# Decoder step on one core: key sums in column groups, late gates from SBUF, three key-value units requested before the root, shorter head and tail, a third-order root

## The chip, the cores and the metric

One Trainium2 chip, one core of it. The metric is the device time of one execution in microseconds. The program has five engines that each run their own queue in order: TensorE (PE) for matrix products, VectorE (DVE), ScalarE (ACT), GpSimd (POOL) and SyncE (SP), which here issues nearly all transfers.

## What is computed

One step of a two-layer decoder for a prompt (16 meta tokens and 256 tokens) and eight sampled tokens, 280 columns in all, in float32. Layer 0 is an RWKV-7 mixer of width 4096 (64 heads of 64), layer 1 windowed attention with a sink per head over keys and values that both token groups compute once from the stream after layer 0. Both have a gate path. Cut to what the change touches:

```python
def rmsnorm(x, g):
    return x * rsqrt(mean(x * x, -1) + RMS_EPS) * g
...
kk = k_h * k_k                                                    # layer 0
kk = kk / maximum(sqrt(sum(kk * kk, axis=-1)), 1e-12)             # one sum per head and token
...
S_fin, y = scan(rwkv7_step, S0, (r, d, k, v, kk, b))
y = (y - mean) * rsqrt(var + GN_EPS) * gn_g + gn_b
y = y + sum(r_h * k_h * r_k, -1) * v_h
y = y.reshape(B, T, WIDTH) * silu(z)                              # the gate
h = h + y @ w_out
...
kv = rmsnorm(h, kv_norm) @ w_kv                                   # shared keys and values
...
y_prompt, y_sample = rmsnorm(h, final_norm)                       # after layer 1
```

## The kernel before

Activations lie with the feature on the partition, 128 rows to a tile, 280 columns (264 in layer 1). A large product is split in three: weights come from DRAM in units of 128x512 (`raw`, two k-tiles by 256 output columns), ACT casts a unit to a short-mantissa type (`whi`), DVE takes the difference (`wlo`), and `mm3` multiplies high by high, high by low and low by high (L207 to L209). Each of `raw`, `whi` and `wlo` has five buffers, so ACT and DVE work a few units ahead of PE.

`phase0` normalises the input: squares of 16 k-tiles (`dx`) on ACT and DVE as the chunks of x land, some added in pairs on DVE, twelve sum matmuls into `ps_ssq` (L324), Ln and Exp on ACT (L346, L347, with a table load between them), and the first products with `raw_k`. Then comes phase A, some 1290 us: products r, k, v, z in order on PE, and between them the chunked solve and state chain of layer 0. For each pair of k-tiles p0 the key sums are two full-width float32 matmuls of the squared keys against a selector (`sel`, L509 in the first four pairs, L814 in the other twelve), which add up four rows of one bank (`ps_kk`); DVE limits them (`ks`) and SP writes four rows to `kr` in DRAM. From L814 on the bank is the only one of its pool (`pp`); the low-rank products `ps_l`, which the ACT instruction `ta` (L862) reads, use the same bank.

A group's normalised output is put into `b = U[u]['bonus']`, the tiles `vT`, and written to `yd` in DRAM (L1240). For most groups the z product's epilogue reads it back (L761). For the two last gate tiles, b = 6 and 7, `gate_a` reads y from `yd` (L1356) and z from `zd`, copies eight sample columns and multiplies four planes (L1362, L1364); `gate_tiles` then casts (`ghi`, `glo`). These late gates fall among the last products `ps_o` of phase A.

`out_a` is the output product of layer 0: for each pair of columns 12 units, the sum with the stream (`hT`), scaled copies for the key-value product (`kvh`, `kvl`), and squares. In between `pump` issues the sampled tokens' state updates: a load, five DVE instructions (L1340 to L1343, 0.68 us each) and a store, at the unit numbers given to `plan_states`. The two last sums go to `ps_sta` (L1414), and ACT makes the root by Ln and Exp (L1416, L1417). `phase_b` begins with the key-value product; its units are requested by `gemm`, behind the root in the code. The scaled copies `bmh` for layer 1 (L1424) are written after it.

`out_b` is layer 1's output product. For each k-tile: sum with the stream, square, three transposes, three multiplies with the final norm's weight (L1831); at the end the sums (`pst`, L1834), `rsqrt` on DVE in ten instructions (L284 to L288), two halves of 1024 columns scaled on DVE and two on ACT, and the output transfers.

The order on each engine is set when the program is built: a planner with a model of each instruction's time issues ready work to each engine; inside `pe_order` blocks the written order holds, and `issue_after` keeps an instruction behind a named one. So an edit can move rows far from it.

## Time and profile before

| | us |
|---|---|
| median of three runs | 2161.58 |
| lowest and highest run | 2156.39, 2165.62 |
| the profiled execution | 2157.39 |
| its span | 2155.6 |
| PE, DVE, ACT busy in the span | 2102.4, 1709.1, 1260.4 |

A row of a timeline gives the start, the duration, the engine, the line of the kernel, the operation, out<-in, shapes and how many records are in it; in brackets stand the engine's idle time before it and what ended that. A float32 matmul leaves two records, one of a split product one. A matmul's duration runs past the start of the next, so PE's pace is read from starts. A row of a table by windows gives the window, its length, busy time (and instructions) of PE, weight loads, DVE, ACT and POOL, then the granted TensorE clock as a share of full speed (1.00 is 2.4 GHz, 0.50 is 1.2), the DMA engines' busy share and GB/s.

### The profile page before, as it was taken

How to read it: one execution, taken by the hardware profiler on the slowest of the kernel's cores; microseconds unless marked ns; L12 is line 12 of the kernel's file. 1: busy time of each engine (PE TensorE's matmuls, PEld its weight loads, DVE VectorE, ACT ScalarE, POOL GpSimd, SP SyncE). 2: the span in 40 equal slices, each digit the busy share in tenths (PEclk: the TensorE clock that was granted, in tenths of full speed). 3: DMA queues.
4: the chain of work that ended last, by engine and by line, in shares of the span. 5: the costliest groups of instructions: out<-in, count | busy, mean ns of one | idle time of the engine just before them, and what ended most of it. 6: DMA issues, size and time to landing. Idle time of an engine off the chain costs nothing.

```text
span 2155.6 us, 56147 instructions
## 1 busy us (share of the span) xinstructions
PE 2102.4 (98%) x21556; PEld 2001.5 (93%) x21556; DVE 1709.1 (79%) x4115; ACT 1260.4 (58%) x2756; POOL 136.4 (6%) x196
## 2 busy tenths in 40 slices
PE   9999999999999999999999999999999999999997
PEld 7999999999898898889989999999999999999997
DVE  7867867787587777888988787897888888878885
ACT  3457756576666666767666444565565565544443
POOL 0011100001010010100101000100000000000000
PEclk9999999999999999999999999999999999999999
DMA  7997667768666775677655778767545444577774
GB/s 252 310 331 244 197 197 237 207 191 274 200 177 183 249 231 168 208 217 205 199 159 199 242 231 250 238 198 232 149 136 167 153 148 137 170 216 239 230 222 133
DMA packets 277445, 448.52 MB, mean 208 GB/s; under 512 B 53352, under 2 KB 99112, under 8 KB 276784
## 3 DMA queue, kind: packets, MB, share of 16 engines
q1 hardware_dynamic: 276888, 443.89, 66.1%
q8 instruction: 169, 2.77, 0.5%
q10 hardware_dynamic: 288, 1.05, 0.1%
q14 instruction: 100, 0.82, 0.1%
HBM read 382.81 MB, written 66.15 MB: 208 GB/s over the span
## 4 chain that ended last, share of the span: by engine, by line
PE 59%; DVE 4%; DMA 2%; ACT 2%; issue 2%; SPq 0%; DVEq 0%; POOLq 0%; ACTq 0%
PE ps_z L207 5%; PE ps_z L208 5%; PE ps_z L209 5%; PE ps_ob L209 3%; PE ps_ob L208 3%; PE ps_ob L207 3%; PE ps_q L207 3%; PE ps_q L209 3%; PE ps_q L208 3%; PE ps_oa L208 2%; PE ps_oa L207 2%; PE ps_oa L209 2%; PE ps_o L207 1%; PE ps_o L209 1%; PE ps_o L208 1%
## 5 line engine op out<-in xcount | busy, mean ns | idle before, releaser
L207 PE MATMUL ps_z<-mhlm,whi_z 128*128 128x280 f32 x512 | 158.2, 309 | 1.1 <-ACT st L771 1.1
L207 PE MATMUL ps_q<-bmh,whi_qb 128*128 128x264 f32 x512 | 149.9, 293 | 0.1
L208 PE MATMUL ps_z<-mhlm,whi_z 128*128 128x280 f32 x512 | 149.6, 292 | 0.0
L209 PE MATMUL ps_z<-mhlm,wlo_z 128*128 128x280 f32 x512 | 149.5, 292 | 0.0
L207 PE MATMUL ps_z<-bmh,whi_zb 128*128 128x264 f32 x512 | 147.5, 288 | 0.0
L209 PE MATMUL ps_q<-bmh,wlo_qb 128*128 128x264 f32 x512 | 145.7, 285 | 0.6 <-DVE wlo_qb L186 0.6
L208 PE MATMUL ps_q<-bml,whi_qb 128*128 128x264 f32 x512 | 145.6, 284 | 0.0
L208 PE MATMUL ps_z<-bml,whi_zb 128*128 128x264 f32 x512 | 145.4, 284 | 0.0
L209 PE MATMUL ps_z<-bmh,wlo_zb 128*128 128x264 f32 x512 | 145.4, 284 | 0.0
L207 PE MATMUL ps_ob<-ghi,whi_ob 128*128 128x264 f32 x512 | 145.2, 284 | 0.0
L209 PE MATMUL ps_ob<-ghi,wlo_ob 128*128 128x264 f32 x512 | 144.8, 285 | 0.0
L208 PE MATMUL ps_ob<-glo,whi_ob 128*128 128x264 f32 x512 | 144.5, 283 | 0.0
L184 ACT CAST whi_ob<-raw_ob 128x512 fp32r<-128x512 f32 x128 | 79.2, 621 | 97.0 <-PE ps_ob L208 80.3
L184 ACT CAST whi_oa<-raw_oa 128x512 fp32r<-128x512 f32 x128 | 79.0, 620 | 89.7 <-PE ps_oa L208 27.1
L186 DVE TENSOR_TENSOR wlo_r<-raw_r,whi_r 128x512 fp32r<-128x512 f32 x128 | 87.2, 686 | 46.9 <-ACT whi_r L184 44.1
L207 PE MATMUL ps_v<-mhlm,whi_v 128*128 128x280 f32 x384 | 120.7, 314 | 0.0
L207 PE MATMUL ps_k<-mhlm,whi_k 128*128 128x280 f32 x384 | 120.1, 313 | 0.0
L184 ACT CAST whi_v<-raw_v 128x512 fp32r<-128x512 f32 x128 | 78.7, 618 | 64.0 <-PE ps_v L208 35.0
L184 ACT CAST whi_zb<-raw_zb 128x512 fp32r<-128x512 f32 x128 | 78.3, 620 | 62.5 <-PE ps_z L208 38.5
L186 DVE TENSOR_TENSOR wlo_v<-raw_v,whi_v 128x512 fp32r<-128x512 f32 x128 | 87.3, 687 | 34.8 <-ACT whi_v L184 31.2
L186 DVE TENSOR_TENSOR wlo_k<-raw_k,whi_k 128x512 fp32r<-128x512 f32 x112 | 76.7, 690 | 46.7 <-ACT whi_k L184 45.8
L186 DVE TENSOR_TENSOR wlo_oa<-raw_oa,whi_oa 128x512 fp32r<-128x512 f32 x128 | 87.1, 688 | 32.5 <-ACT whi_oa L184 29.5
(461 smaller groups left out, 7747.3 us busy)
## 6 DMA issues: line engine op xcount, KB each, us to landing
raw_k<-a_w_rkvz SPq DMA_DIRECT2D x128, 256.0 KB
raw_v<-a_w_rkvz SPq DMA_DIRECT2D x128, 256.0 KB
raw_r<-a_w_rkvz SPq DMA_DIRECT2D x128, 256.0 KB
raw_z<-a_w_rkvz SPq DMA_DIRECT2D x128, 256.0 KB
raw_oa<-a_w_out SPq DMA_DIRECT2D x128, 256.0 KB
raw_qb<-b_w_qz SPq DMA_DIRECT2D x128, 256.0 KB
raw_zb<-b_w_qz SPq DMA_DIRECT2D x128, 256.0 KB
raw_ob<-b_w_o SPq DMA_DIRECT2D x128, 256.0 KB
```

The source lines that it names most:

```text
L184: self.nc.scalar.copy(hi, src)
L186: return self.nc.vector.tensor_tensor(lo, src, hi.bitcast(F32), op=ALU.subtract)
L207: mm(ps, wh, xh, start=start, stop=False)
L208: mm(ps, wh, xl, start=False, stop=False)
L209: return mm(ps, wl, xh, start=False, stop=stop)
```

## The change

Seven edits. `phase0` adds more squares in pairs on DVE, so that eight sum matmuls are left. The key sums' selector has 32 columns instead of 128, and the two matmuls of a pair write rows 0 to 31 and 32 to 63 of the bank, each on its own; `ks` covers 64 rows and two transfers of two rows replace one of four. `rsqrt` takes one third-order step and one second-order step instead of three second-order ones: eight instructions for ten. The late gates multiply z with `vT` in SBUF, in three instructions for five, and groups 6 and 7 are no longer written to `yd` nor read. `out_a` requests three key-value units before the root's Ln. The state updates stand at other unit numbers. In `out_b` the last k-tile's sums stand ahead of its transposes, its multiplies with the final norm's weight are merged with the root's, and the first scaled piece is 512 columns wide. (The edit of `end_k` is that of `squares`; `gemm` takes the units that `out_a` has begun.)

```diff
@@ -263,10 +264,9 @@
-        selt = self.cp.tile([128, 130], F32, name="selt")
-        nc.gpsimd.memset(selt, 0.0)
-        dma(selt[:, 2:4], I['consts'][:, C_SEL:C_SEL + 2])
-        self.sel = [selt[:, 2:130], selt[:, 0:128]]
+        self.sel = self.cp.tile([128, 32], F32, name="selt")
+        nc.gpsimd.memset(self.sel, 0.0)
+        dma(self.sel[:, 0:2], I['consts'][:, C_SEL:C_SEL + 2])
         self.half = self.cp.tile([128, 2], F32, name="half")
@@ -282,10 +282,14 @@
         V.tensor_scalar(y.bitcast(I32), x.bitcast(I32), -0.5, 1597463007.0, op0=MU, op1=AD)
-        for i in range(3):
-            V.tensor_tensor(t, y, y, op=MU)
-            V.scalar_tensor_tensor(t, t, -0.5, x, op0=MU, op1=MU)
-            V.scalar_tensor_tensor(x if i == 2 else y, t, 1.5, y, op0=AD, op1=MU)
+        STT = V.scalar_tensor_tensor
+        V.tensor_tensor(t, y, y, op=MU)
+        V.tensor_tensor(t, t, x, op=MU)
+        STT(t, t, -10 / 3, t, op0=AD, op1=MU)
+        STT(y, t, 5.0, y, op0=AD, op1=MU)
+        V.tensor_tensor(t, y, y, op=MU)
+        STT(t, t, -27 / 1024, x, op0=MU, op1=MU)
+        STT(x, t, 9 / 16, y, op0=AD, op1=MU)
@@ -311,7 +315,7 @@
         vsq = lambda a, b: V.tensor_tensor(sq[:, a:b], xn[:, a:b, :N], xn[:, a:b, :N], op=MU)
-        add = lambda a, b: V.tensor_tensor(sq[:, a:a + 2], sq[:, a:a + 2], sq[:, b:b + 2], op=AD)
+        add = lambda a, b, n=2: V.tensor_tensor(sq[:, a:a + n], sq[:, a:a + n], sq[:, b:b + n], op=AD)
         pss, junk = (self.bank(self.pe, n) for n in ("ps_ssq", "ps_fill"))
@@ -336,13 +340,15 @@
             vsq(10, 12)
-            summed(8, 9, 10, 11)
             asq(12, 13)
             vsq(13, 14)
-            summed(12, 13)
-            asq(14, 15)
-            vsq(15, 16)
-            summed(14, 15)
+            add(12, 13, 1)
+            summed(12)
+            add(8, 10)
+            summed(8, 9)
+            asq(14, 16)
+            add(14, 15, 1)
+            summed(14)
             A.activation(rsb, pss[:, :N], AF.Ln, scale=1.0 / D, bias=self.epst)
@@ -506,10 +512,12 @@
         for j in range(2):
-            nc.tensor.matmul(pk[:, :N], self.sel[j], sqs[j], start=j == 0, stop=j == 1)
-        ks = self.ph.tile([128, N], F32, tag="ks0", name=f"ks{p0}")[:4]
-        nc.vector.tensor_scalar(ks, pk[:4, :N], 1e-24, None, op0=ALU.max)
-        nc.sync.dma_start(self.kr[p0 // 8][2 * p0 % 16:2 * p0 % 16 + 4], ks)
+            nc.tensor.matmul(pk[32 * j:32 * j + 32, :N], self.sel, sqs[j], start=True, stop=True)
+        ks = self.ph.tile([128, N], F32, tag="ks0", name=f"ks{p0}")[:64]
+        nc.vector.tensor_scalar(ks, pk[:64, :N], 1e-24, None, op0=ALU.max)
+        for j in range(2):
+            h = 2 * (p0 + j) % 16
+            nc.sync.dma_start(self.kr[p0 // 8][h:h + 2], ks[32 * j:32 * j + 2])
         if p0 == 6:
@@ -1236,7 +1246,7 @@
                                    op0=MU, op1=AD)
-            if j % 2:
+            if j % 2 and o < GZ // 2:
                 nc.sync.dma_start(self.yd[u // 2][:, 2 * (u % 2):2 * (u % 2) + 2, :L], b[:, :, :L])
@@ -1353,15 +1363,15 @@
             z = pool.tile([128, 4, N], F32, tag="gz", bufs=bufs, name=f"gz{b}")
-            nc.sync.dma_start(y[:, :, :L], self.yd[b][:, :, :L])
             nc.sync.dma_start(z, self.zd[b])
         else:
             nc.sync.dma_start(y, self.yd[b])
         ys = self.ys[:, 4 * b:4 * b + 4]
         if late:
-            nc.vector.tensor_copy(y[:, :, L:N], ys)
-            for pl in range(4):
-                nc.vector.scalar_tensor_tensor(y[:, pl], z[:, pl], 0.5, y[:, pl], op0=ALU.mult, op1=ALU.mult)
+            nc.vector.scalar_tensor_tensor(y[:, :, L:N], z[:, :, L:N], 0.5, ys, op0=ALU.mult, op1=ALU.mult)
+            for i in range(2):
+                s, v = slice(2 * i, 2 * i + 2), self.U[2 * b + i]['bonus']
+                nc.vector.scalar_tensor_tensor(y[:, s, :L], z[:, s, :L], 0.5, v[:, :, :L], op0=ALU.mult, op1=ALU.mult)
         else:
@@ -1391,7 +1401,7 @@
         self.wx = self.wx0
-        self.plan_states(self.st0, 0, range(12, 96, 7), 5)
+        self.plan_states(self.st0, 0, [*range(10, 60, 6), 74, 81, 88], 5)
         ones = pool.tile([128, 128], F32, name="ones")
@@ -1413,6 +1423,8 @@
                                  stop=k == KT - 1)
+        units = self.wunits(self.I['w_kv'][0], "kv", KT, 0, 256, 2)
+        self.kvu = itertools.chain([next(units) for _ in range(3)], units)
         nc.scalar.activation(self.rb, pst[:, :N], AF.Ln, bias=self.epst, scale=1.0 / D)
@@ -1455,7 +1467,7 @@
                 if c % 2 == 0:
-                    pss = self.gemm(I['w_kv'][0], "kv", KT, c * 128, x)
+                    pss = self.gemm(I['w_kv'][0], "kv", KT, c * 128, x, units=None if c else self.kvu)
                     self.pump(c == 2)
@@ -1797,6 +1809,10 @@
+    def stb(self, pst, rows, a, one, first):
+        for i, r in enumerate(rows):
+            self.nc.tensor.matmul(pst[i][:r, 0:2], a[:, 128 * i:128 * i + r], one, start=first, stop=not first)
+
     def out_b(self):
@@ -1824,28 +1840,37 @@
             pt = self.bank(self.pe, f"ps_h2_{k}")
+            if k == KT - 1:
+                self.stb(pst, rows, sq, one, False)
             for i, r in enumerate(rows):
                 nc.tensor.transpose(pt[:r, 128 * i:128 * i + 128], h[:, 128 * i:128 * i + r], self.ident)
-            for i, r in enumerate(rows):
+            for i, r in enumerate(rows[:3 if k < KT - 1 else 0]):
                 s = slice(128 * k, 128 * k + 128)
                 V.tensor_tensor(ht[i][:r, s], pt[:r, 128 * i:128 * i + 128], fn[:r, s], op=ALU.mult)
-            if k >= KT - 2:
-                for i, r in enumerate(rows):
-                    nc.tensor.matmul(pst[i][:r, 0:2], (acc if k == KT - 2 else sq)[:, 128 * i:128 * i + r], one,
-                                     start=k == KT - 2, stop=k == KT - 1)
+            if k == KT - 2:
+                self.stb(pst, rows, acc, one, True)
         rs = pool.tile([128, 3], F32, name="rsf")
         V.memset(rs, 1.0)
         for i, r in enumerate(rows):
             V.tensor_scalar(rs[:r, i:i + 1], pst[i][:r, 0:1], 1.0 / D, EPS, op0=ALU.mult, op1=ALU.add)
         self.rsqrt(rs, pool)
         outs = (O['y_prompt'][0, 0:128], O['y_prompt'][0, 128:256], O['y_sample'].rearrange("b o d -> (b o) d"))
-        for c in range(2):
-            s = slice(D // 2 * c, D // 2 * c + D // 2)
-            V.tensor_scalar(ht[0][:, s], ht[0][:, s], rs[:, 0:1], None, op0=ALU.mult)
-            nc.sync.dma_start(outs[0][:, s], ht[0][:, s])
+        last = slice(D - 128, D)
+        scaled = lambda i, s: V.tensor_scalar(ht[i][:, s], ht[i][:, s], rs[:, i:i + 1], None, op0=ALU.mult)
+        ends = lambda i, r: V.scalar_tensor_tensor(ht[i][:r, last], pt[:r, 128 * i:128 * i + 128], rs[:r, i:i + 1],
+                                                   fn[:r, last], op0=ALU.mult, op1=ALU.mult)
+        for a, b in ((0, 512), (512, 1280), (1280, 2048)):
+            s = slice(a, min(b, D - 128))
+            scaled(0, s)
+            if b == D:
+                ends(0, 128)
+            nc.sync.dma_start(outs[0][:, a:b], ht[0][:, a:b])
             A.activation(ht[1][:, s], ht[1][:, s], AF.Copy, scale=rs[:, 1:2])
-            nc.scalar.dma_start(outs[1][:, s], ht[1][:, s])
-        V.tensor_scalar(ht[2][:NS], ht[2][:NS], rs[:NS, 2:3], None, op0=ALU.mult)
+            if b == D:
+                ends(1, 128)
+            nc.scalar.dma_start(outs[1][:, a:b], ht[1][:, a:b])
+        V.tensor_scalar(ht[2][:NS, :D - 128], ht[2][:NS, :D - 128], rs[:NS, 2:3], None, op0=ALU.mult)
+        ends(2, NS)
         nc.sync.dma_start(outs[2], ht[2][:NS])
```

What it does to the order of instructions, in three places.

DVE, phase A, round the first key sum of the third block (`ks` frees the bank for `ps_l`; `kk` and `cl` are a product and a scan that prepare another group). Before:

```order
L999 TENSOR_TENSOR RB_11396<-ps_sc_9_11574,consts 64x2x128
L186 TENSOR_TENSOR wlo_k_12_11733<-raw_k_12_11730,whi_k_12_11732 128x512
L877 SCALAR_TENSOR_TENSOR kk_11786<-kT_11782,par,kk_11786 128x280 x2
L889 SCALAR_TENSOR_TENSOR cl_11454<-reset,cl_11454 128x272 x2
L816 TENSOR_SCALAR ks_11610<-ps_kk_11607 4x280
L186 TENSOR_TENSOR wlo_k_14_11773<-raw_k_14_11770,whi_k_14_11772 128x512
```

After:

```order
L1009 TENSOR_TENSOR RB_11392<-ps_sc_9_11568,consts 64x2x128
L824 TENSOR_SCALAR ks_11604<-ps_kk_11601 64x280
L187 TENSOR_TENSOR wlo_k_12_11728<-raw_k_12_11725,whi_k_12_11727 128x512
L887 SCALAR_TENSOR_TENSOR kk_11781<-kT_11777,par,kk_11781 128x280 x2
L899 SCALAR_TENSOR_TENSOR cl_11448<-reset,cl_11448 128x272 x2
L187 TENSOR_TENSOR wlo_k_14_11768<-raw_k_14_11765,whi_k_14_11767 128x512
```

`ks` has moved ahead of a weight difference, two products and two scans.

ACT, the last products of phase A (`ghi` is the cast of a gate tile, the two of b = 6 and b = 7; `whi_oa_1792` are the weights of the last but one product, `whi_oa_0` and on those of `out_a`). Before:

```order
L184 CAST whi_oa_1792_2_20416<-raw_oa_1792_2_20414 128x512
L184 CAST whi_oa_1792_4_20441<-raw_oa_1792_4_20439 128x512
L184 CAST ghi_20349<-gy_20340 128x1120
L184 CAST whi_oa_1792_6_20447<-raw_oa_1792_6_20445 128x512
L184 CAST whi_oa_1792_8_20477<-raw_oa_1792_8_20475 128x512
L184 CAST whi_oa_1792_10_20495<-raw_oa_1792_10_20493 128x512
L184 CAST whi_oa_1792_12_20513<-raw_oa_1792_12_20511 128x512
L184 CAST whi_oa_1792_14_20531<-raw_oa_1792_14_20529 128x512
L184 CAST whi_oa_0_20597<-raw_oa_0_20595 128x512
L184 CAST whi_oa_2_20603<-raw_oa_2_20601 128x512
L184 CAST whi_oa_4_20633<-raw_oa_4_20631 128x512
L184 CAST ghi_20404<-gy_20395 128x1120
```

After:

```order
L185 CAST whi_oa_1792_0_20360<-raw_oa_1792_0_20358 128x512
L185 CAST ghi_20325<-gy_20319 128x1120
L185 CAST whi_oa_1792_2_20388<-raw_oa_1792_2_20386 128x512
L185 CAST whi_oa_1792_4_20413<-raw_oa_1792_4_20411 128x512
L185 CAST ghi_20376<-gy_20370 128x1120
L185 CAST whi_oa_1792_6_20419<-raw_oa_1792_6_20417 128x512
L185 CAST whi_oa_1792_8_20449<-raw_oa_1792_8_20447 128x512
L185 CAST whi_oa_1792_10_20467<-raw_oa_1792_10_20465 128x512
L185 CAST whi_oa_1792_12_20485<-raw_oa_1792_12_20483 128x512
```

The cast of b = 6 has moved ahead of two weight casts and that of b = 7 ahead of eight.

ACT, the root between `out_a` and the key-value product (`rb` is the root, `bmh` a scaled copy for layer 1). Before:

```order
L1417 ACT_TABLE_LOAD
L1417 ACTIVATE rb<-rb 128x280
L1424 ACTIVATE bmh_22815<-hT,par 128x280
L1424 ACTIVATE bmh_22819<-hT,par 128x280
L1424 ACTIVATE bmh_22823<-hT,par 128x280
L184 CAST whi_kv_14_22156<-raw_kv_14_22154 128x512
L1424 ACTIVATE bmh_22827<-hT,par 128x280
L184 CAST whi_kv_0_22227<-raw_kv_0_22225 128x512
```

After:

```order
L1429 ACT_TABLE_LOAD
L1429 ACTIVATE rb<-rb 128x280
L1436 ACTIVATE bmh_22787<-hT,par 128x280
L1436 ACTIVATE bmh_22791<-hT,par 128x280
L1436 ACTIVATE bmh_22795<-hT,par 128x280
L1436 ACTIVATE bmh_22799<-hT,par 128x280
L185 CAST whi_kv_14_22135<-raw_kv_14_22133 128x512
L185 CAST whi_kv_0_22200<-raw_kv_0_22198 128x512
```

`whi_kv_14`, the eighth unit, stands behind the Exp in both, after the change behind four `bmh` instead of three; `whi_kv_0` of the next columns follows it directly.

## Rows read from the trace of the kernel before

**Rows 1.** The page, part 1: busy time, share of the span and instructions of each engine.

```profile
PE 2102.4 (98%) x21556; PEld 2001.5 (93%) x21556; DVE 1709.1 (79%) x4115; ACT 1260.4 (58%) x2756; POOL 136.4 (6%) x196
```

**Rows 2.** The forms of the key-sum matmuls (durations are shortest, median, longest, in ns), and PE's timeline round one pair of them.

```profile
L814 PE MATMUL ps_kk<-sqk,selt x48: 398/399/503, 296.7 to 806.7; 128*128 128x280 f32 x48
...
L509 PE MATMUL ps_kk<-sqp,selt x16: 397/398/399, 50.7 to 79.5; 128*128 128x280 f32 x16
...
769.76 0.29 PE L209 MATMUL ps_k<-mhlm,wlo_k 128*128 128x280 f32 x1
769.89 1.11 PE L814 MATMUL ps_kk<-sqk,selt 128*128 128x280 f32 x4
...
770.97 0.29 PE L208 MATMUL ps_k<-mhlm,whi_k 128*128 128x280 f32 x1
```

**Rows 3.** The chain of work that ended last, in layer 1: start, time on the chain, engine, tile, line and records. L1726 are float32 matmuls of 256 columns into the upper and the lower 64 rows of the output, in turn, L1728 the same of 128 columns; x4 are two matmuls.

```profile
1516.74 0.58 PE ps_at L1726 x4
1517.32 0.22 PE ps_at L1728 x4
1517.54 0.43 PE ps_at L1726 x4
```

**Rows 4.** PE's timeline: a product, and behind it float32 matmuls that use 64 of the 128 rows.

```profile
301.22 0.29 PE L209 MATMUL ps_k<-mhlm,wlo_k 128*128 128x280 f32 x1
301.44 0.64 PE L1006 MATMUL ps_sc<-E,KB 64*128 64x32 f32 x8
```

**Rows 5.** The timeline of DVE, SP, PE and ACT round the first key sum of the third block, and PE's window behind it.

```profile
753.63 0.92 DVE L877 SCALAR_TENSOR_TENSOR kk<-kT,par,kk 128x280 f32<-128x280 f32 x2
...
754.47 1.32 DVE L889 TENSOR_TENSOR_SCAN cl<-reset,cl 128x272 f32<-128x272 f32 x2
...
755.72 0.41 DVE L816 TENSOR_SCALAR ks<-ps_kk 4x280 f32<-4x280 f32 x1
...
756.16 0.27 SPq L817 DMA_DIRECT2D kr<-ks  x1
...
756.18 0.40 PE L207 MATMUL ps_l<-lt5h,lhi 96*128 96x280 f32 x1 [2.66 <-DVE ks L816]
...
757.07 0.48 ACT L862 ACTIVATE ta<-ps_l,par 128x280 f32<-128x280 f32 x1
...
757.00:759.00 2.00, 2.00 (x10) 2.00 (x10) 0.66 (x4) 1.47 (x5) 2.00 (x4) 0.50 0.52 140
```

**Rows 6.** The timeline of DVE, ACT, SP and PE round the late gates, and the table by windows ahead of it and there.

```profile
1299.14 1.53 DVE L1364 SCALAR_TENSOR_TENSOR gy<-gz,gy 128x280 f32<-128x280 f32 x4 [2.56 <-issue]
...
1300.70 1.12 ACT L184 CAST ghi<-gy 128x1120 fp32r<-128x1120 f32 x1 [5.56 <-DVE gy L1364]
...
1302.14 0.58 SPq L1356 DMA_DIRECT2D gy<-yd  x1
...
1302.40 0.40 PE L207 MATMUL ps_o<-mhlm,whi_oa 128*128 128x280 f32 x1 [1.99 <-ACT whi_oa L184]
...
1303.84 0.60 PE L209 MATMUL ps_o<-mhlm,wlo_oa 128*128 128x280 f32 x1 [0.92 <-DVE wlo_oa L186]
...
1286.00:1290.00 4.00, 4.00 (x35) 4.00 (x34) 3.95 (x8) 1.37 (x3) 0.00 (x0) 1.00 1.02 351
...
1302.00:1306.00 4.00, 2.68 (x11) 2.46 (x12) 3.65 (x5) 2.68 (x5) 0.00 (x0) 0.60 1.01 334
1306.00:1310.00 4.00, 4.00 (x20) 4.00 (x19) 3.06 (x8) 1.28 (x3) 0.00 (x0) 0.55 1.00 369
```

**Rows 7.** The timeline of ACT and PE at the root between `out_a` and the key-value product.

```profile
1418.87 0.50 ACT L1416 ACTIVATE rb<-ps_sta,epst 128x280 f32<-128x280 f32 x1 [0.27 <-PE ps_sta L1414]
...
1423.16 1.28 ACT L1417 ACT_TABLE_LOAD   x1
...
1426.06 0.60 ACT L184 CAST whi_kv<-raw_kv 128x512 fp32r<-128x512 f32 x1
...
1426.72 0.40 PE L207 MATMUL ps_kv<-kvh,whi_kv 128*128 128x280 f32 x1 [1.45 <-ACT whi_kv L184]
```

**Rows 8.** The timeline of PE and ACT in `phase0`: the last sum matmuls, Ln, and the first product.

```profile
11.70 1.34 PE L324 MATMUL ps_ssq<-dx,ones 128*128 128x280 f32 x5
...
13.08 0.49 ACT L346 ACTIVATE rsb<-ps_ssq,epst 128x280 f32<-128x280 f32 x1 [3.32 <-PE ps_ssq L324]
...
17.09 1.21 PE L242 MATMUL ps_k<-mst,raw_k 128*128 128x280 f32 x4 [0.74 <-DVE mst L374]
```

**Rows 9.** The timeline of DVE in the tail (a last multiply, a step of `rsqrt`, the scaling of two halves), and the table by windows behind it.

```profile
2143.34 0.68 DVE L1831 TENSOR_TENSOR ht<-ps_h,fn 128x128 f32<-128x128 f32 x3 [0.68 <-PE ps_h L1828]
...
2144.45 0.16 DVE L286 TENSOR_TENSOR rst<-rsy 128x3 f32<-128x3 f32 x1
...
2146.22 1.42 DVE L1844 TENSOR_SCALAR ht<-ht,rsf 128x1024 f32<-128x1024 f32 x2
...
2148.00:2152.00 4.00, 0.00 (x0) 0.00 (x0) 0.82 (x1) 0.40 (x1) 0.00 (x0) 0.50 1.01 404
```

**Rows 10.** PE's timeline at its longest stop, the ten microseconds round it, and a stretch of `out_a`, by windows.

```profile
933.39 1.48 PE L1079 MATMUL ps_so<-TN,Noff 32*32 32x16 f32 x128 [4.05 <-DVE TN L1058]
...
930.00:940.00 10.00, 6.61 (x221) 6.41 (x222) 5.37 (x15) 4.38 (x7) 0.77 (x2) 0.83 0.82 261
1350.00:1400.00 50.00, 50.00 (x389) 50.00 (x388) 45.42 (x74) 26.03 (x48) 8.59 (x8) 1.00 0.78 239
```

More of the change, by code (lines that the diff above doesn't have):

```diff
@@ L2 @@
 import functools
+import itertools
 import numpy as np
@@ L209, in mm3, with gemm @@
         return mm(ps, wl, xh, start=False, stop=stop)
-    def gemm(self, w, name, nk, col, x, n=N, ncol=256, per=2):
+    def gemm(self, w, name, nk, col, x, n=N, ncol=256, per=2, units=None):
         parts = range(0, ncol, 128)
@@ L215, in gemm @@
         out = [p[:min(128, ncol), :n] for p in ps]
-        units = self.wunits(w, name, nk, col, ncol, per)
+        units = units or self.wunits(w, name, nk, col, ncol, per)
         for two in zip(units, units):
@@ L323, in summed @@
             for k in ks:
-                nc.tensor.matmul(pss[:, :N], ones, sq[:, k], start=k == 0, stop=k == KT - 1)
+                nc.tensor.matmul(pss[:, :N], ones, sq[:, k], start=k == 0, stop=k == KT - 2)
         eng = mybir.EngineType
@@ L813, in end_k @@
         for j in range(2):
-            nc.tensor.matmul(pk[:, :N], self.sel[j], sq[:, j], start=j == 0, stop=j == 1)
-        ks = sp.tile([128, N], F32, tag="sqp", bufs=1, name=f"ks{p0}")[:4]
-        nc.vector.tensor_scalar(ks, pk[:4, :N], 1e-24, None, op0=ALU.max)
-        nc.sync.dma_start(self.kr[p0 // 8][2 * p0 % 16:2 * p0 % 16 + 4], ks)
+            nc.tensor.matmul(pk[32 * j:32 * j + 32, :N], self.sel, sq[:, j], start=True, stop=True)
+        ks = sp.tile([128, N], F32, tag="sqp", bufs=1, name=f"ks{p0}")[:64]
+        nc.vector.tensor_scalar(ks, pk[:64, :N], 1e-24, None, op0=ALU.max)
+        for j in range(2):
+            h = 2 * (p0 + j) % 16
+            nc.sync.dma_start(self.kr[p0 // 8][h:h + 2], ks[32 * j:32 * j + 2])
         self.mark('x', 1, p0)
```

## The prediction

> **What bounds the kernel now.** First the page: TensorE (PE) is busy 98% of the span [rows 1]. That is 2102.4 of 2155.6 us; the last matmul ends near 2144, so about 12 of the missing 53 us are the tail after it (its root stands at 2144.45 [rows 9]) and about 41 are stops in between. So only four things can move the time: fewer PE microseconds, a shorter head or tail, a stop of PE taken away, or half-clock time taken away. What DVE, ACT, POOL and SP gain or lose counts only where PE waits for them. Then the forms of the key-sum matmuls and PE's timeline round one pair [rows 2], with two places that price column groups [rows 3, 4]. Then, for each stop that the change touches, the timeline of the stop and the granted clock behind it [rows 5 to 7]; then head and tail [rows 8, 9]; last the rows for the opposite case [rows 10]. In the last set the reader is to see that a long stop is paid twice: 4.05 us of idle stand before 933.39, and the ten microseconds round it were granted 0.83 of full speed.
>
> **Key sums in two column groups.** 48 and 16 records [rows 2], two records to a matmul, are 32 matmuls, 16 pairs. A pair starts at 769.89; the second product behind it starts at 770.97, products being 0.13 apart, so a pair costs 770.97 - 769.89 - 0.13 = 0.95 us. The chain shows what two matmuls into different column halves cost [rows 3]: two of 256 columns take 0.58 and then 0.43 us together. At the pair's own pace (0.95 / 2 / 280 columns = 1.7 ns a column) two of 256 one after another would take 0.87. So they ran side by side, and the first time 0.15 was added. Another change from full to smaller tiles shows the same cost: the small matmul starts 0.22 us after the product before it, not 0.13 [rows 4], so 0.09. Side by side a pair costs 0.47 and saves 0.47; I charge 0.14 of that for the change of form as a whole, so 0.33 is left, and 15 pairs give 5.0 us (in the remaining pair, p0 = 4, a product still stands between the two matmuls: nothing). Bounds: no cost of the change of form, 16 x 0.47 = 7.5; 0.15 each way, 15 x 0.17 = 2.6; not side by side, 0. I take **-5.0**, since a cost of entering is shown in both places and one of leaving in neither. The Trainium skill, "TensorEngine Tiling (Array Packing)", section "Key Properties", says that a change of the tiling mode, not just of the tile, drains the engine; the 0.15 in [rows 3] agrees in sign. By that rule, with a drain both ways, the sum would have -2.6 here, by side-by-side running alone -7.5.
>
> Each pair now issues two writes to DRAM instead of one: 16 more SP issues of 0.27 us [rows 5]. They wait for nothing that the single one did not wait for, and the weight loads queued behind them are several units ahead of use. Cost taken: 0, up to 0.3 us each if PE were waiting for a load there.
>
> **An unwritten effect: the key sum's evacuation moves.** PE stopped 2.66 us before 756.18 for the bank that `ks` frees [rows 5]; DVE ran `ks` only after two `kk` products (0.92), two scans (1.32) and a weight difference. The new order has `ks` ahead of all of them (order, first place), so it ends about 2.4 us earlier, before PE gets there. The clock was at half behind the stop (0.50 from 757 to 759, the last of [rows 5]); behind the stop at 933.39 ten microseconds at a mean of 0.83 are (1 - 0.83) x 2 x 10 = 3.4 us at half, 1.7 lost [rows 10], and I take the same here. The gain is 2.66 + 1.7 = 4.4 at most. What is late next: the same bank is wanted again 18 products and ten small matmuls later, about 3 us, and is then freed by `ta`, which stood at 757.07 behind scans that the move pushes back by 0.4; with `ks` at 753 that second use comes near 756.9 and may wait 0.5 to 1. I take **-3.0**, bounds 0 (a stop of the same size a little later) and -4.4.
>
> **Late gates.** The last gate tile but one waited for its rows to come back from DRAM: DVE's products began at 1299.14, the cast `ghi` at 1300.70 after 5.56 us idle, and PE stopped 1.99 and 0.92 us for weight casts queued behind it [rows 6]. The clock then stood at half: 0.60 and 0.55 over eight microseconds mean (0.40 + 0.45) x 2 x 4 = 6.8 us at half, of which 0.9 idle, so 3.0 lost. Together 5.9. After the change those products read vT in SBUF and need only z, whose load stands well ahead in SP's order; the order has both gates' products, and both casts, well ahead of the weight casts that PE waited for (order, second place). Two reads and four writes, SP's with 0.58 us for a read, leave the queue at a place where the DMA engines are full (share 1.01, 1.00). Three DVE instructions replace a copy and four products: no dearer. Cover if the gates are early: DVE had 0.05 us free between 1286 and 1290 [rows 6], so one gate's 1.5 us goes there at the cost of a later weight difference. I take **-5.5**; bounds -2.9 (only the idle time or only the clock comes back) and -5.9.
>
> **Key-value weights ahead of the root.** Both orders already have seven key-value units cast before the table load of the root; the eighth stays behind it, and after the change one more `bmh` stands ahead of it (order, third place). PE's stop of 1.45 us is the chain from Ln at 1418.87 through nine scaled casts, the table load of 1.28, Exp, three more casts and the weight cast at 1426.06 [rows 7]; one `bmh` more is +0.43, and the unit behind the eighth comes that much sooner. So it does not do what it says here: **0**, bounds +0.5 and -2.0 (the 1.45 and its neighbours gone). The state steps start at 10 and stand 6 units apart instead of 7, off the last columns: DVE was busy 45.4 of 50 us in that stretch [rows 10], and 3.4 us of steps each 9.2 instead of 10.8 us make it 0.96 of the time, still under PE: 0.
>
> **Head.** Four of twelve sum matmuls go. Five records took 1.34 us to 13.04, Ln began at 13.08 and the first product followed 4.0 later [rows 8]. Eight records fewer would be 8 x 0.24 = 1.9 us if PE alone set the end; but the last chunk lands no sooner, and its square is now followed by an add on DVE (about 0.45 for 280 columns, from `kk`'s 0.92 for two [rows 5]) with another of 560 ahead of it (0.74 by the same pace): 1.9 - 0.45 and up to 0.9 of queueing: **-1.0**, bounds -0.5 and -1.3. **Root and tail.** 10 steps become 8, 0.2 us each between 2144.45 and 2146.22; three multiplies (0.68) no longer stand ahead of the root; the first scaled piece is 512 wide instead of 1024 (1.42 for two, so 0.35 sooner) [rows 9]. That is 0.4 + 0.3 + 0.35 = 1.05 until the first output leaves, and from there the transfer bounds (404 GB/s): **-1.0**, bounds -0.6 and -1.4. The other 16 roots lie beside PE's work: 0.
>
> **The sum.** -5.0 - 3.0 - 5.5 + 0 - 1.0 - 1.0 = -15.5. The profiled execution took 2157.39 us (span 2155.6 and 1.8 round it), so it would take 2141.9. It lies 4.2 below the median of the runs, 2161.58; the same difference from the median gives **2146.1**. Adding the small ends of all bounds gives -2.6 - 2.9 + 0.5 - 0.5 - 0.6 = -6.1, the large ends -7.5 - 4.4 - 5.9 - 2.0 - 1.3 - 1.4 = -22.5: 2155.5 and 2139.1.
>
> **Rivals.** (A) as summed, 2146. (B) The two matmuls do not run side by side: the first term is 0 and the sum -10.5, 2151. For it: the halves in [rows 3] are 64 wide, these 32, and a tile of 32 beside another is in no row; against it: 0.43 for two. (C) The stops move instead of going. For it: DMA share 1.01 and a full DVE before the gates, and `ta` behind the scans; then gates and `ks` give 1 each and the sum is -9.0, 2152.6. (D) B and C together: -4.0, 2157.6. (E) Slower: the planner has moved DVE and ACT rows round some forty places before 1290. The solver's stops are of that kind: PE waits for one transpose, `TN`, at 933.39, and one such stop costs 4.05 idle and about 1.7 of clock [rows 10]. In the new order one `TN` of another group stands four rows later on DVE. Each new stop costs 2.4 to 5.8; from three new ones the gain of A is gone, and with six (26 us) the time is 2172. Against it: PE's own order there is unchanged, and most rows move by one place.
>
> **How the numbers follow.** A 0.56, B 0.11, C 0.17, D 0.10, E 0.06. 0.5% is 10.8 us, about what a measurement can tell from no change. A is faster by more than that, bar its own small end; B lies on the line and is split; C and D are within; E is slower. Faster 0.61, same 0.33, slower 0.06. The range reaches from A's large end to D: 2139 to 2158.
>
> **What would show it.** A pair near 0.62 us on PE (0.95: B; 0.47: no cost of the change of form). No idle time above 1 us before the ps_l behind the third block's first key sum. Granted clock 1.00 from 1290 to 1310, `ghi` of both late gates before the weight casts of their product. The 1.45 before the eighth key-value unit still there, up to 1.9. Ln of the head near 12, and the first output about 1 us sooner after the last transposes. New stops over 2 us before 1290 would make the prediction wrong, as would a time above 2158.

## The result, and the profile after

The changed kernel took **2144.47 us** (median of 9 runs, 2142.16 to 2157.84), the kernel before 2157.56 in the same series (9 runs, 2155.26 to 2165.62): ratio **0.994, 95% interval 0.9923 to 0.9957**, so 9 to 17 us faster. The forecast was 2146.1, 15.5 under a median of 2161.58; in this series the change took 13.1 off 2157.56. The profiled execution took 2148.06, of which the span is 2146.2.

PE is still what bounds it. The page, part 1, answers to [rows 1]:

```profile
PE 2098.6 (98%) x21548; PEld 1993.0 (93%) x21548; DVE 1705.8 (79%) x4080; ACT 1260.3 (59%) x2757; POOL 137.0 (6%) x196
```

The span fell by 9.4 us and PE's busy time, which half clock lengthens, by only 3.8, so more than half of the gain between these two executions is idle time of PE: stops, head and tail. To find the places, put the start of each matmul beside the start of the same matmul in the trace before (both counted from the first one) and take the median difference round a time. This is worked out from the traces, one profiled execution each; a minus is ahead of the kernel before, a plus behind it, and the times at the top are those of the kernel before.

```
time before, us      30   100   340   430   640   740   840  1250  1340  1520
changed kernel     -0.6  -0.4   0.0  +6.4  +2.8  +5.3  -1.2  -5.3  -7.9  -8.6
same, once more    -0.9  -0.7  -1.3  +5.4  +1.9  +1.2  -4.2  -6.8 -12.5 -14.6
shorter root alone  0.0   0.0  +1.1  +9.9  +8.7  +9.7  +7.8  +4.4  +1.3  +1.0
root, kk held      -0.2  -0.2  +2.4  +1.4  -0.9  +0.2  -3.2  -6.8  -8.1  -8.8
key sums alone     +0.3  +0.4  +0.1  +2.4  -1.3  -0.3  -3.5  -5.6  -8.0  -8.1
old key sums       -1.1  -1.1  +2.8  +8.0  +6.0  +7.9  +4.8  +1.9  -3.4  -4.1
late gates alone   -0.1  -0.1  +3.8  +4.0  +3.0  +4.5  +6.2  +3.0  -1.9  -2.1
changed, kk held   -1.3  -1.1  +0.9  +1.3  -2.3  -3.3  -9.2 -12.8 -18.5 -20.6
```

The first row says that the kernel lost 6.4 us between 340 and 430 and won it back, and more, behind 430. The other rows are the experiments below ("old key sums" is the changed kernel with full-width key sums, "changed, kk held" the changed kernel with `kk` back in its old place). The first two rows are the same program: 6 us apart at the end, and "late gates alone" is 4 us behind at 340, where its rows still stand as in the kernel before. So a single place of one trace is good to a few us at best.

**The stop that nobody forecast.** DVE's timeline of the kernel before at this place:

```profile
374.94 1.12 DVE L1058 STREAM_TRANSPOSE TN<-NL 128x512 f32<-128x512 f32 x1
375.98 0.67 DVE L1059 STREAM_TRANSPOSE TR<-NL 128x512 f32<-128x512 f32 x1
377.02 0.94 DVE L877 SCALAR_TENSOR_TENSOR kk<-kT,par,kk 128x280 f32<-128x280 f32 x2 [0.37 <-DMA kk<-kr]
...
378.47 0.49 DVE L1237 SCALAR_TENSOR_TENSOR vT<-ps_yt,par,vT 128x272 f32<-128x272 f32 x1
```

and DVE, PE and the table by windows of the kernel after:

```profile
378.83 0.93 DVE L887 SCALAR_TENSOR_TENSOR kk<-kT,par,kk 128x280 f32<-128x280 f32 x2 [3.51 <-DMA kk<-kr]
...
382.99 1.03 DVE L1068 STREAM_TRANSPOSE TN<-NL 128x512 f32<-128x512 f32 x1
383.95 0.66 DVE L1069 STREAM_TRANSPOSE TR<-NL 128x512 f32<-128x512 f32 x1
384.54 0.45 DVE L1247 SCALAR_TENSOR_TENSOR vT<-ps_yt,par,vT 128x272 f32<-128x272 f32 x1
...
385.05 0.55 PE L1246 MATMUL ps_yt<-consts,Y 128*128 128x128 f32 x3 [4.02 <-DVE vT L1247]
...
380.00:390.00 10.00, 5.98 (x103) 5.60 (x104) 8.63 (x17) 8.04 (x17) 2.13 (x4) 0.83 0.43 129
```

The same rows in another order: `kk` needs key norms that come back from DRAM. Before, it stood behind the solver's two transposes, and DVE waited 0.37 us for it; now it stands ahead of them, DVE waits 3.51 us, and `vT`, which empties the bank that PE wants, is queued behind it, the scans and the transposes. PE stops for 4.02 us and gets 0.83 of the clock in those ten microseconds.

**Key sums.** PE's timeline round the pair of [rows 2], and the forms:

```profile
770.94 0.29 PE L210 MATMUL ps_k<-mhlm,wlo_k 128*128 128x280 f32 x1
771.16 0.67 PE L822 MATMUL ps_kk<-sqk,selt 128*32 128x280 f32 x4
771.75 0.40 PE L208 MATMUL ps_k<-mhlm,whi_k 128*128 128x280 f32 x1
771.99 0.29 PE L209 MATMUL ps_k<-mhlm,whi_k 128*128 128x280 f32 x1
...
L822 PE MATMUL ps_kk<-sqk,selt x48: 399/411/423, 297.3 to 810.0; 128*32 128x280 f32 x48
L515 PE MATMUL ps_kk<-sqp,selt x16: 399/411/423, 50.2 to 78.9; 128*32 128x280 f32 x16
```

From the product ahead to the second one behind, 771.99 - 770.94 = 1.05; less two products at 0.13, a pair costs 0.79, where it cost 0.95. Of that, 0.22 - 0.13 = 0.09 is going in, 0.52 are two steps of 0.26 each, in which two records run at once, and what is left, 0.18, is coming out.

**The third block's `ks`**, answering to [rows 5]: it now stands ahead of `kk` and the scans, PE starts `ps_l` with no idle time, and the clock is whole.

```profile
757.37 0.43 DVE L824 TENSOR_SCALAR ks<-ps_kk 64x280 f32<-64x280 f32 x1
...
758.47 0.29 PE L208 MATMUL ps_l<-lt5h,lhi 96*128 96x280 f32 x1
...
757.00:759.00 2.00, 2.00 (x20) 1.94 (x20) 1.99 (x6) 0.97 (x3) 0.00 (x0) 1.00 0.25 93
```

**Late gates**, answering to [rows 6]. `ghi` no longer comes late, but PE stops again nearby, for the bank that `xr` frees:

```profile
1275.71 0.86 DVE L774 TENSOR_TENSOR xr<-ps_o,xr 128x280 f32<-128x280 f32 x2
...
1281.05 0.19 DVE L1376 SCALAR_TENSOR_TENSOR gy<-ys,gy 128x32 f32<-128x32 f32 x1 [1.16 <-DMA gy<-yd]
...
1291.21 0.71 DVE L1374 SCALAR_TENSOR_TENSOR gy<-gz,vT 128x544 f32<-128x544 f32 x1
...
1292.45 0.80 DVE L774 TENSOR_TENSOR xr<-ps_o,xr 128x280 f32<-128x280 f32 x2
...
1292.94 0.40 PE L208 MATMUL ps_o<-mhlm,whi_oa 128*128 128x280 f32 x1 [2.11 <-DVE xr L774]
...
1290.00:1300.00 10.00, 7.89 (x49) 7.67 (x48) 7.86 (x12) 4.68 (x7) 0.00 (x0) 0.83 0.97 312
```

The row at 1281.05 is the last of the gates that still read their rows from DRAM. From its start to that of `xr` are 11.40 us, in which DVE is never idle.

**Root, head and tail**, answering to [rows 7 to 9]: nine `bmh` casts still stand between Ln and the table load, and PE waits 1.77 for the eighth unit; Ln of the head starts at 12.52 and the first product at 16.52, which is 0.56 and 0.57 earlier; the first output leaves at 2137.40.

```profile
1411.23 3.88 ACT L1436 ACTIVATE bmh<-hT,par 128x280 fp32r<-128x280 f32 x9
1415.12 1.28 ACT L1429 ACT_TABLE_LOAD   x1
...
1419.09 0.40 PE L208 MATMUL ps_kv<-kvh,whi_kv 128*128 128x280 f32 x1 [1.77 <-ACT whi_kv L185]
...
12.52 0.49 ACT L352 ACTIVATE rsb<-ps_ssq,epst 128x280 f32<-128x280 f32 x1 [2.06 <-PE ps_ssq L328]
...
16.52 1.68 PE L243 MATMUL ps_k<-mst,raw_k 128*128 128x280 f32 x6 [0.74 <-DVE mst L380]
...
2132.98 0.43 DVE L1834 TENSOR_TENSOR h<-ps_ob,hT 128x264 f32<-128x264 f32 x1 [1.02 <-PE ps_ob L210]
...
2137.40 1.58 SPq L1867 DMA_DIRECT2D y_prompt<-ht  x3
```

From the last `h` to the end are 2146.2 - 2132.98 = 13.22 us; the same two points of the trace before give 2155.6 - 2141.65 = 13.95. The first output leaves 4.42 behind the last `h` and left 5.35 behind it, so 0.2 of the 0.9 is lost again behind it.

### The profile page after: what moved, and what is told of

Its sections match the earlier page's. It is cut to its first block, busy times and chain, and to the rows that moved or that the text cites. A ratio compares the mean times of both kernels' runs of the same rounds, so it can differ in the third digit from the quotient of the medians.

```text
span 2146.2 us, 56094 instructions
## 1 busy us (share of the span) xinstructions
PE 2098.6 (98%) x21548; PEld 1993.0 (93%) x21548; DVE 1705.8 (79%) x4080; ACT 1260.3 (59%) x2757; POOL 137.0 (6%) x196
## 3 DMA queue, kind: packets, MB, share of 16 engines
q10 hardware_dynamic: 432, 1.05, 0.1%
## 4 chain that ended last, share of the span: by engine, by line
PE 85%; DVE 5%; DMA 4%; ACT 3%; issue 2%; SPq 0%; POOL 0%; DVEq 0%; POOLq 0%; ACTq 0%
PE ps_z L208 6%; PE ps_z L209 6%; PE ps_z L210 6%; PE ps_r L208 3%; PE ps_ob L208 3%; PE ps_ob L210 3%; PE ps_v L208 3%; PE ps_ob L209 3%; PE ps_q L208 3%; PE ps_q L210 3%; PE ps_q L209 3%; PE ps_k L208 3%; PE ps_r L209 3%; PE ps_r L210 3%; PE ps_v L209 3%; PE ps_v L210 3%
## 5 line engine op out<-in xcount | busy, mean ns | idle before, releaser
L208 PE MATMUL ps_v<-mhlm,whi_v 128*128 128x280 f32 x384 | 121.2, 316 | 1.4 <-ACT st L779 1.4
L208 PE MATMUL ps_k<-mhlm,whi_k 128*128 128x280 f32 x384 | 120.0, 312 | 1.3 <-ACT st L779 1.3
L209 PE MATMUL ps_k<-mhlm,whi_k 128*128 128x280 f32 x384 | 112.5, 293 | 0.0
L209 PE MATMUL ps_v<-mhlm,whi_v 128*128 128x280 f32 x384 | 112.5, 293 | 0.0
```

The lines of the kernel that those rows point to most:

```text
L208: mm(ps, wh, xh, start=start, stop=False)
L209: mm(ps, wh, xl, start=False, stop=False)
```

## Experiments

Each was timed beside the kernel before on the same chip (medians of before 2159.78, 2157.86 and 2156.32 in three series, the last on another chip: both held, one to a unit, the root with `kk` held, the second issue). Between series only ratios are compared. Ratios are against it, with 95% intervals. In the expectations, "record" is the prediction, and the letters O, M, X, N and G are explanations, each spelt out where it first stands; B is the rival of the prediction.

**The changed kernel once more** (no edit).

> The changed kernel once more. Theory O (its new stops are written into the order of its rows): TensorE stops again for about 4.0 us near 385 (vector engine held by kk, whose rows are not yet back from DRAM), 2.2 near 682 and 2.1 near 1293, and the time is again 13 us under the kernel before (ratio 0.994). Rival N (these stops hang on when a transfer happens to land): the stop near 385 is under 1 us in this profile and its span is 4 to 6 us shorter than 2146.2.

2145.05, ratio 0.9939 (0.9919 to 0.996). The stop near 385 recurred with 3.84 us: it belongs to the order of the rows, not to the moment. The one near 682, ended by a copy of ACT, was 1.22 (2.22 above). The one for `xr` shrank to 0.60, with the clock whole. Its rows beside those above:

```profile
1274.41 0.87 DVE L774 TENSOR_TENSOR xr<-ps_o,xr 128x280 f32<-128x280 f32 x2
...
1277.95 0.19 DVE L1376 SCALAR_TENSOR_TENSOR gy<-ys,gy 128x32 f32<-128x32 f32 x1 [1.56 <-DMA gy<-yd]
...
1289.36 0.80 DVE L774 TENSOR_TENSOR xr<-ps_o,xr 128x280 f32<-128x280 f32 x2
...
1289.85 0.40 PE L208 MATMUL ps_o<-mhlm,whi_oa 128*128 128x280 f32 x1 [0.60 <-DVE xr L774]
```

From `gy` to `xr` 11.41 us again; but `gy` follows the `xr` ahead of it by 3.54 us here and by 5.34 above. In two further kernels with these rows in the same order it is 3.99 (stop 1.26) and 2.98 (no stop over 0.6). So what still ends last is a read from DRAM, that of the gate ahead, carried to PE by a full DVE queue. Theory O holds near 385, N near 1293.

**The shorter root alone.**

```diff
-        for i in range(3):    # 9 instructions, in the kernel before
+        V.tensor_tensor(t, y, y, op=MU)    # ... the 7 of the change
```

> The kernel before with the shorter root alone, everywhere it is used. Record (the 16 roots inside lie beside other work, the last one gives 0.4): 0.4 us faster than before, no new stop. Theory O: a shorter root makes the planner put kk of the second block ahead of the solver's two transposes TN and TR near 375, the vector engine then waits there for kk's rows, and TensorE stops 3 to 6 us near 385 with half clock behind it: 3 to 6 us slower than before (2161 to 2164 against 2157.6). Rival N: within 1 us of before.

2158.86, ratio 1.0006 (0.999 to 1.0021). So O has the stop right and the time wrong: not 3 to 6 us slower, but no difference that can be told. The stop is there, without any other part of the change:

```profile
379.41 0.93 DVE L881 SCALAR_TENSOR_TENSOR kk<-kT,par,kk 128x280 f32<-128x280 f32 x2 [4.75 <-DMA kk<-kr]
380.25 1.07 DVE L1062 STREAM_TRANSPOSE TN<-NL 128x512 f32<-128x512 f32 x1
...
385.57 0.90 PE L1240 MATMUL ps_yt<-consts,Y 128*128 128x128 f32 x3 [4.67 <-DVE vT L1241]
```

It set this kernel back 8.8 us (table, 340 to 430), but at the end it was only 1.0 behind. Something gave 9 us later; what, the run on the root with `kk` held tells.

**Key sums in two column groups alone.**

```diff
-            nc.tensor.matmul(pk[:, :N], self.sel[j], sqs[j], start=j == 0, stop=j == 1)
+            nc.tensor.matmul(pk[32 * j:32 * j + 32, :N], self.sel, sqs[j], start=True, stop=True)
```

> The kernel before with the key sums in two column groups alone. Record: pairs -5.0 and the third block's key-sum bank -3.0, so 8 us faster (2149.6 against 2157.6). Theory M (each pair gives 0.16 to 0.36, not 0.33 to 0.47; the stop of 2.66 near 756 goes with its clock): -2.3 and -4.2, 6.5 faster, 2151; less by what new order stops cost, here kk again ahead of TN near 375 but behind the scans: up to 3 of it, 2154. Rival B (no side by side): 4 faster, stop gone, pair 0.95 or more.

2155.26, ratio 0.9979 (0.9964 to 0.9993): 4.5 us, between M's two figures, 6.5 and 3.5. `kk` stands ahead of TN here too, behind the scans, and PE stops 2.44 at 382: the shorter root is enough to move `kk`, but it is not the only edit that does.

**The changed kernel with full-width key sums** (the same lines the other way).

> The changed kernel with the old full-width key sums. Record: 8 us slower than the changed kernel (2152.5 against 2144.5). Theory M: 6.5 slower (2151), the stop for the bank that ks frees back near 755 (2 to 3 us), and the stop near 385 still there, since it comes from the root. Rival: the stop near 385 comes from the two writes of a pair instead of one; then it is gone here and the time is 2145 to 2147.

2151.45, ratio 0.9964 (0.995 to 0.9978): 6.4 us above the changed kernel in the same series (5.4 by the ratios, good to some 5), as M had it. The stop near 385 is still there (3.41), so the second write of a pair does not make it. The stop for `ks`, though, is smaller than M had it, with `ks` behind `kk` and the scans; why, no run tells:

```profile
762.39 0.40 PE L208 MATMUL ps_l<-lt5h,lhi 96*128 96x280 f32 x1 [1.00 <-DVE ks L823]
```

**`kk` held behind TN and TR.**

```diff
+        with self.tc.issue_after(self.last_tr.ins) if u == 4 else contextlib.nullcontext():
             for j in range(2):
                 V.scalar_tensor_tensor(kk[:, j], kT[:, j], self.pcol(P_KK, p0 + j), ...
```

> The changed kernel with one order restored: kk of the second block stands behind the solver's TN and TR again, as in the kernel before. Theory O: the stop near 385 (3.8 to 4.0 us, with clock 5 to 6.6) goes; if nothing gives it back later the time is 2138 to 2140. Rival G (time lost early is given back later, since waits that a transfer ends shrink when TensorE comes late: with the shorter root alone it stood 10 us behind the kernel before at 540 and 1 us at the end): the stop goes, the waits near 680, 820 to 930 grow by 2 to 4, and the time is 2141 to 2144.

2136.88, ratio **0.9904** (0.9881 to 0.9926): 7.6 us under the changed kernel's median, 7.8 by the two ratios, good to some 6. Of the kernels near it, the one below with this hold and that of the last gate has 0.9903, and the three without this hold have 0.994, 0.9939 and 0.9929. The stop is gone, and nothing took it back: the table's last row gains 6.3 on the second one between 340 and 430 (+0.4 against +6.7), and is 6.0 ahead of it at the end. O holds, G falls.

**The last gate held behind `xr`.**

```diff
+            with self.tc.issue_after(self.los[-1].ins) if b == 7 else contextlib.nullcontext():
                 nc.vector.scalar_tensor_tensor(y[:, :, L:N], z[:, :, L:N], 0.5, ys, ...
-            yield (6 if b == G1 else 3), self.after(4, ('g', b))
+            yield (6 if b == G1 else 12 if b == 7 else 3), self.after(4, ('g', b))
```

> The changed kernel with the three products of the last gate held behind the weight difference that follows xr. The first profile of the changed kernel lost 2.11 us near 1293 and clock behind it, the second 0.6 and no clock. Theory X (the vector engine's queue from the read of the gate before, 11.4 us without a gap, decides when xr frees the bank): 1.6 us of that queue now stands behind xr, so the stop is under 0.3 and the clock 1.00 from 1285 to 1300; 0.6 to 3.7 us faster than the changed kernel, 2142 in the middle. Rival: the transfers (share 1.04 there) hold the next weights, the stop returns elsewhere before 1310 with 1 us or more and the time stays.

2142.6, ratio 0.9929 (0.9909 to 0.995), not to be told from the changed kernel. No stop over 0.6 us stands there, but in the kernel with `kk` held none did either, without this edit. And with both:

**Both held.**

> The changed kernel with the two held orders (kk behind TN and TR, the last gate behind xr), the casts bmh where they were. Theory O and X: 7.6 and 1 to 2 together, 2134 to 2137, no stop over 1 us near 385 and 1293, the one of 1.77 near 1419 as before. Rival: what the held kk gave was this run's transfers; then 2140 to 2143.

2134.06, inside the expected 2134 to 2137; but the ratio, 0.9903 (0.988 to 0.9927), is the same as with `kk` alone. The stop for `xr` is back with 0.96, since DVE now waits there for a cast of ACT:

```profile
1280.99 0.69 DVE L187 TENSOR_TENSOR wlo_oa<-raw_oa,whi_oa 128x512 fp32r<-128x512 f32 x1 [1.34 <-ACT whi_oa L185]
1281.60 0.80 DVE L774 TENSOR_TENSOR xr<-ps_o,xr 128x280 f32<-128x280 f32 x2
```

X fits what sets the stop in the order of the changed kernel (four traces above); that this edit gains anything is not shown.

**Both, and the `bmh` casts behind the eighth key-value unit**, five in a row and then three to a unit; then one to a unit.

```diff
+        with self.tc.issue_after(self.his["kv", ...].ins) if tag == "bm" else contextlib.nullcontext():
             self.nc.scalar.activation(hi, self.hT[:, k], AF.Copy, scale=g)
```

> Both of these, and the sixteen scaled casts bmh held behind the eighth key-value unit and the next three. Theory O and X with the record's reading of the root (nine bmh between Ln and the table load make the stop near 1419): that stop of 1.77 goes as well, the three add up, and the time is 2134 to 2139. Rival G: 2139 to 2144.

> The same, and the scaled casts bmh held again, but one behind each key-value unit, not five in a row. With five in a row the stop of the eighth unit went (2.9 us ahead at 1410) and the vector engine's five bml in a row ahead of a weight difference gave a stop of 2.82 and clock in its place (4.9 us lost by 1420). If that is the cause, neither stop stands here and the time is 1 to 3 us under that of the kernel without this hold, 2132 to 2135; rival: the vector engine has no room for one bml a unit (it was busy 5.00 of 5 us there) and a stop of over 1 us stands between 1410 and 1440 all the same.

2140.49, ratio 0.9917 (0.9898 to 0.9936), and 2141.01, ratio 0.992 (0.9901 to 0.994): both above the kernel without this hold, by 3.0 and 3.7 us of ratio, which the intervals alone don't tell from nothing. The traces say the same: from 1250 to 1520 the kernel without it gains 6.9 us on the kernel before, these two 4.2 and 4.0. The eighth unit's stop went in both, so the nine casts are what makes it. A longer one came behind it (2.82 in the first). PE's and DVE's rows of the second:

```profile
1431.85 0.60 PE L213 MATMUL ps_kv<-kvh,wlo_kv 128*128 128x280 f32 x1 [3.85 <-DVE wlo_kv L189]
...
1425.00:1430.00 5.00, 2.41 (x15) 1.74 (x13) 4.85 (x15) 0.04 (x1) 0.00 (x0) 1.00 0.74 189
1430.00:1435.00 5.00, 3.15 (x13) 3.15 (x14) 4.97 (x14) 0.65 (x2) 0.00 (x0) 0.59 0.25 89
```

Each `bmh` is followed by a `bml` on DVE, and DVE, busy 4.85 and 4.97 of 5 us, has no room for them there. So the 1.77 us at the eighth unit were the cheaper side in these traces. The rival of the second expectation holds.

**Late gates alone.**

```diff
-            nc.vector.tensor_copy(y[:, :, L:N], ys)
+            nc.vector.scalar_tensor_tensor(y[:, s, :L], z[:, s, :L], 0.5, v[:, :, :L], ...   # v is vT in SBUF
```

> The kernel before with the late gates from SBUF alone. Record: 5.5 us faster (2152 against 2157.6), bounds 2.9 and 5.9. Theory X: the stops of 1.99 and 0.92 near 1303 go and one of 0.6 to 2.1 for xr stands in their place, 2.5 to 5.9 faster as the profiled transfers land; before 1270 no difference over 0.5 us from the kernel before.

2153.05, ratio 0.9976 (0.9961 to 0.9991): 4.8 us faster, and in its trace 4.9 between 1250 and 1340, with a stop of 1.55 for `xr`. That nothing moves before 1270 was wrong in this one trace (+4.5 at 740); its rows there are in the old order.

**The shorter root, with `kk` held.**

> The kernel before with the shorter root, and kk of the second block held behind TN and TR as in the kernel before. With the root alone TensorE was 8.5 us behind at 380 and 1.0 behind at the end, so 7.5 came back. Theory O: the stop of 4.67 near 385 goes, 6 to 8.5 with it. If the shorter root itself gives what came back (less work on the vector engine between 780 and 1050, against the record, which put the 16 roots inside at 0), the time is 5 to 8 us under before, 2150 to 2153. If it came back only because TensorE was late (rival G), the time is that of before less the last root's 0.4, 2157.

2152.49, ratio 0.998 (0.9965 to 0.9994): 1.5 to 7.5 us faster than before, where 5 to 8 were expected, and 5.6 under the root alone by the two ratios (1.0006 - 0.998 = 0.0026, good to some 5 us). Its `kk` waits 0.70 and PE does not stop there. Both rows of the table with the root fall by 5 to 7 us between 740 and 1250, late or not, where that of the late gates alone falls by 1.5; so rival G falls here too. Less the last root's 0.4, the shorter root, with the order that comes with it, gives some 4 us inside the program (1 to 7 by the interval).

**Each pair's two matmuls issued a second time**, into column groups 2 and 3.

```diff
+        for j in range(2):
+            nc.tensor.matmul(pk[64 + 32 * j:96 + 32 * j, :N], self.sel, sqs[j], start=True, stop=True)
```

> The changed kernel with each pair's two matmuls issued a second time into column groups 2 and 3 (the same sums once more, into rows that nobody reads): eight records a pair, not four. A pair now costs 0.79 us of TensorE (1.05 from the product before it to the second one behind it, less two products at 0.13), of which 0.52 are two passes of 0.26, each over both groups at once. If a pass runs in all four groups at once and the rest is the change of form: 0.79 again, within 0.03, and the time within 1 us of the changed kernel. If groups run two at a time: 1.31 a pair, 16 x 0.52 = 8 us slower. If each further matmul only costs its start: some 0.01 to 0.05 a pair.

```profile
766.92 0.29 PE L210 MATMUL ps_k<-mhlm,wlo_k 128*128 128x280 f32 x1
767.14 0.43 PE L824 MATMUL ps_kk<-sqk,selt 128*32 128x280 f32 x2
767.15 0.43 PE L826 MATMUL ps_kk<-sqk,selt 128*32 128x280 f32 x2
767.40 0.41 PE L824 MATMUL ps_kk<-sqk,selt 128*32 128x280 f32 x2
767.41 0.41 PE L826 MATMUL ps_kk<-sqk,selt 128*32 128x280 f32 x2
767.75 0.40 PE L208 MATMUL ps_k<-mhlm,whi_k 128*128 128x280 f32 x1
767.98 0.29 PE L209 MATMUL ps_k<-mhlm,whi_k 128*128 128x280 f32 x1
```

767.98 - 766.92 - 0.26 = 0.80 for eight records, where four cost 0.79: all four groups run at once. The whole was expected within 1 us of the changed kernel and took 2149.29, ratio 0.9967 (0.9954 to 0.998), about 6 us more by the ratios, which the price of a pair doesn't explain. Its stop near 385 was 5.86 in this trace; whether that is the whole reason stays open.

## Why the prediction came out right

The total came out right, in part by luck. The forecast took 15.5 us off a median of three runs, 2161.58; the change took 13.1 off 2157.56, the median of nine. A gain 2.4 smaller and a base 4.0 lower leave the 1.6 between 2146.1 and 2144.47. Of the terms, the place and the direction were right, two sizes were not, and two effects that were not in the sum, a new stop and what the shorter root gives inside, cancelled in part.

Of the signs that the prediction named, these came: no idle time before the third block's `ps_l`, both `ghi` early, the eighth unit's wait, Ln near 12, the first output 0.9 sooner. A pair is 0.79, between A's 0.62 and B's 0.95. The clock from 1290 to 1300 was 0.83 in the first profile and 1.00 in the second. And the sign that was to make it wrong, new stops over 2 us before 1290, is there twice: 4.02 at 385.05, and this one of 2.22, which no run explains (1.22 in the second profile, none at this line with the root alone or the keys alone):

```profile
682.38 1.03 PE L1188 MATMUL ps_wu<-W,TT 64*64 64x64 f32 x16 [2.22 <-ACT W L1180]
```

- **Key sums, -5.0, mis-sized: -2.9.** Place by place, from the product ahead to the third one behind, the two traces differ by 0.15 to 0.16 at ten of 17 places, 0.35 at three with small solver tiles behind, 0.36 and 0.51 at two that wait for operands; the pair with a product between its matmuls costs 0.31 more, twice. Summed, -2.9. Side by side was right (B falls), but I charged 0.14 for the change of form once; it is 0.09 in and 0.18 out, the two steps take 0.26 each and not 0.24, and the split pair, taken at nothing, pays the change twice. I wrote that a cost of leaving is shown in neither place of the rows. It is, in the two rows behind those of [rows 4]: the first two products behind the small matmuls start 0.23 apart, not 0.13.

```profile
302.00 0.40 PE L207 MATMUL ps_k<-mhlm,whi_k 128*128 128x280 f32 x1
302.23 0.30 PE L208 MATMUL ps_k<-mhlm,whi_k 128*128 128x280 f32 x1
```

  The 0.15 for entering [rows 3] is in part the chain's way of counting: from start to start those two pairs of matmuls take 0.48 and 0.43 us. The Trainium skill, "TensorEngine Tiling (Array Packing)", section "Key Properties", has a drain at each change of the tiling mode. These traces agree, with 0.09 in and 0.18 out, and the -2.6 which the forecast gave by that rule was nearer than its own choice.
- **`ks`, -3.0.** Between 740 and 770 the changed kernel gains 4.2 and 4.7 us in its two profiles, 0.3 of it two pairs. Mechanism and place were right. But the kernel with the old key sums, and `ks` in its old place, gains 3.1 there as well, so not all of it is the move. The key sums alone, with `ks` moved ahead in the same way, gain 2.7 there and leave a stop of 0.67.
- **Late gates, -5.5, mis-sized, with C's mechanism.** The rows for both stops went. One of 0.6 to 2.1 for `xr` came instead, and the gain between 1250 and 1340 was 2.6 and 5.7 (alone 4.9; by its runs 4.8). The clock was over-charged too: the same old stops (1.93 and 0.91; 2.02 and 0.78) were followed by a granted clock of 1.00 in the profiles of the root alone and the keys alone, where [rows 6] has 0.60 and 0.55. Eight microseconds of the table by windows round them, first of the one, then of the other:

```profile
1306.00:1314.00 8.00, 6.79 (x50) 6.57 (x51) 6.20 (x11) 3.87 (x8) 0.00 (x0) 1.00 0.99 327
```

```profile
1296.00:1304.00 8.00, 6.78 (x50) 6.55 (x51) 4.99 (x8) 2.86 (x5) 0.00 (x0) 1.00 1.02 331
```

  I took 3.0 us from one execution for something that some executions don't pay.
- **Key-value weights, 0:** the eighth unit's wait is there, 1.77, in the range said; the waits of 0.67 and 0.66 behind it went, and between 1340 and 1520 the two profiles gain 0.7 and 2.1. **Head, -1.0:** -0.6 and -0.9 (the 0.74 for an add of 560 columns doesn't follow from `kk`'s pace, which gives 0.92; the trace has 0.74). **Root and tail, -1.0:** 13.95 - 13.22 = -0.7.
- **The step that failed: "the other 16 roots lie beside PE's work: 0."** Four of them make the key norms that `kk` waits for. With all roots two instructions shorter, `kk` moved ahead of TN (shown by the root alone), and that cost 6 to 8 us: a stop of the kind that rival E feared, dearer than its 2.4 to 5.8. The column groups alone move `kk` too, with a stop of 2.44; that it is the four key-norm roots and not the other twelve is likely and not shown. Inside, the shorter root also gave some 4 us (1 to 7). The prediction weighed moved rows as stops of the solver alone, and no row that waits for a transfer.

Sum of what was measured by part, each by its ratio of 2157: keys -4.5, gates -5.2, root with its stop +1.3 (the tail's two steps in it), head and the rest of the tail some -1.1: -9.5. The key-value units were not run alone. The whole is -13, within what intervals of 3 us on each part allow; the parts also share stops, so they need not add.
